# A SwiGLU feed-forward on one core: two products moved behind residual steps, and a fourth PSUM bank for the down product

## The chip, the cores and the metric

The kernel runs on one core of a Trainium2 chip. The metric is the device time of one execution in microseconds (us). Five engines work side by side: PE multiplies matrices (PEld is its weight load), DVE, ACT and POOL work element by element, and SP issues DMAs. PE writes its results into PSUM, which holds 8 banks of 128 partitions x 512 fp32 values; DVE and ACT read them from there.

## The reference, cut to what matters

The program is one decoder block: adaLN modulation, two token mixers (a gated recurrence and a dilated attention), an output projection, a SwiGLU feed-forward, and a final RMSNorm. SEQ is 2048, D_MODEL is 1024 and D_FF is 2816. The change touches the part from the feed-forward on (and one helper that the norms before it use as well):

```python
h = modulate(rms_norm(x, norm2_g[l]), shift2, scale2)
a, u = jnp.split(h @ w_gate_up[l], 2, axis=-1)
x = x + gate2[:, None, :] * ((jax.nn.silu(a) * u) @ w_down[l])
...
return rms_norm(x, final_g)
```

## The kernel before, in words

**Precision.** Every fp32 operand is split into a high part and a low part (`whi`, `wlo` for weights, `ahi`, `alo` for activations, `chi`, `clo` for the feed-forward's input), and a product is three matmuls: high x high, low x high, high x low. The weight split is a cast on ACT (L277) and a subtraction on POOL (L79, `wlo`).

**Blocks and pairs.** The 2048 tokens are cut into six blocks of 344 or 336 tokens (`n`), taken as three pairs (the loop `p`). The two blocks of a pair and the two halves of D_MODEL make a 2 x 2 block product, which `gate_up` computes with seven products instead of eight (a Strassen scheme); its sums and differences of the input are the `pieces` `h["11"]`, `h["S1"]` and so on, made by DVE and ACT.

**Columns and downs.** For each pair there are eleven steps `g`. Each runs `gate_up` for two columns of 128 gate and 128 up features. A column ends in `finish`, twice (once for each block): DVE multiplies silu(gate) by up (`tt(dve, si, si, u, ALU.mult)`, shown in the trace as DVE `hm<-hm`), and `two_parts` splits that product into `ahi` (ACT, L291) and `alo` (DVE). For the second column of a pair the splits are put into a list `late` and called later, inside the next `down`.

**The down product.** `down(g - 1, ...)` multiplies the two columns of the step before by the down weights. It has 16 steps, one for each 128-row tile of the output and each block. A step is six matmuls (L1123, L1124, L1125, twice) into one PSUM tile `psD`, and then one DVE instruction (L1126, the residual step) that reads `psD` and adds it into `xc`. The tag `psD` has three banks, so the fourth step's first matmul can only start when the residual step of the first has read its bank. In all there are 33 downs of 16 steps.

**The norms.** `norm_sum` (L296) sums squares over the partitions by a matmul with a matrix of ones into a PSUM tile `nps`, in a bank of its own. It serves the norms of the output projection, and the final norm: twice within the downs of the second and third pair, and twice in the last down. The products of `gate_up` have four banks (`psG`). Together that is all eight banks.

**Order.** The program is written in Python in one order, and a scheduler then puts each engine's instructions in an order of its own, by when it expects their inputs to be ready. Each engine then works through its list strictly in that order.

Of the kernel before, what the change touches and what calls it, by code (L numbers as in the profile page):

```python
# [10 lines left out]
F32 = mybir.dt.float32  # L11
# [4 lines left out]
ALU = mybir.AluOpType  # L16
# [3 lines left out]
P = 128  # L20
# [9 lines left out]
CH = 512  # L30
# [19 lines left out]
def hybrid_block(ctx, tc, xT, small, cst, w_ada, w_ft, w_tk, w_out, w_gu, w_dn, out):  # L50
    nc = tc.nc
    act, dve, pool, pe = nc.scalar, nc.vector, nc.gpsimd, nc.tensor
# [25 lines left out]
    def tt(eng, o, a, b, op):  # L78
        return eng.tensor_tensor(o, a, b, op)  # L79
# [173 lines left out]
    cpool, silu = {}, []  # L253

    def c_pool(name, stack=cx, **kw):
        cpool[name] = stack.enter_context(tc.tile_pool(name=name, bufs=1, reuse_waits="tile", **kw))
        return cpool[name]
# [11 lines left out]
    def raw_w(src):  # L269
        raw = cpool["wp"].tile([P, 512], F32, name="wraw", tag="wraw", bufs=7)  # L270
        nc.sync.dma_start(out=raw, in_=src)
        return raw
# [8 lines left out]
    def split(src, eng=pool):  # L281
        return [parts(raw_w(src[:, z * 512:(z + 1) * 512]), eng=eng) for z in range(2)]
# [6 lines left out]
    def two_parts(dst, src, eng=dve, copy=act.copy):  # L289
        hi, lo = dst  # L290
        copy(hi, src)  # L291
        tt(eng, lo, src, hi.bitcast(F32), ALU.subtract)

    def norm_sum(ssq, n):
        ps = cpool["pp_n"].tile([P, CH], F32, name="nps", tag="nps", bufs=1)[:, 0:n]
        pe.matmul(ps, ones, ssq, start=True, stop=True)  # L296
        return ps

# [26 lines left out]
    with ExitStack() as ab:  # L325
# [88 lines left out]
        with tc.tile_pool(name="ada0", bufs=2) as pl:  # L414
# [18 lines left out]
            with tc.manual_schedule(engines={mybir.EngineType.PE}):  # L433
              done = {}
              for k in range(KT + LAG0):
# [4 lines left out]
                  if 0 < k <= KT:  # L440
                      n = k - 1
# [435 lines left out]
    def product(ps, w, h, start=True, stop=True):  # L877

        for k, (hi, lo) in enumerate(h):
            ws = slice(k * P, (k + 1) * P)  # L880
            pe.matmul(ps, w[0][:, ws], hi, start=start and k == 0, stop=False, skip_group_check=True)  # L881
            pe.matmul(ps, w[0][:, ws], lo, start=False, stop=False, skip_group_check=True)  # L882
            last = pe.matmul(ps, w[1][:, ws], hi, start=False, stop=stop and k == 3, skip_group_check=True)  # L883
        return last.ins

    def psG(n):
        return cpool["ppc"].tile([P, CH], F32, name="psG", tag="psG", bufs=4)[:, 0:n]
# [45 lines left out]
    with ExitStack() as wl:  # L933
        for nm in ("hg1", "at0", "xw0", "xw1", "at1", "wsc"):
            c_pool(nm, wl)
        for nm in ("pp_d", "ppc", "pp_n"):
            c_pool(nm, space=PSUM)

        def w_tile(name, bufs=2):
# [39 lines left out]
        for i, (c, j) in enumerate(order):  # L979
# [5 lines left out]
            if begun:  # L985
                ps = begun.pop(0)
            else:
                ps = psG(CH)
# [26 lines left out]
            if c == NCH - 1:  # L1015
# [3 lines left out]
                if j == 1:  # L1019
                    n = BLK[0][1]  # L1020
# [13 lines left out]
    with cx:  # L1034
        for nm in ("wk_h", "wk_a", "wkc", "xpc0", "xpc1"):
            c_pool(nm)
        pp_d, wk_a = cpool["pp_d"], cpool["wk_a"]

        def hm(n):
            return cpool["wk_h"].tile([P, T], F32, name="hm", tag="hm", bufs=6)[:, 0:n]  # L1040

        def a_tile(n):
            return tuple(wk_a.tile([P, T], F32R, name=nm, tag=nm, bufs=8)[:, 0:n] for nm in ("ahi", "alo"))
# [9 lines left out]
        def gate_up(f, h, n, wait=False):  # L1053


            b11, b12 = raw_w(w_gu[f][:, 0:512]), raw_w(w_gu[FT + f][:, 0:512])
            b22, b21 = raw_w(w_gu[FT + f][:, 512:1024]), raw_w(w_gu[f][:, 512:1024])
            t1, t2 = [cpool["wk_h"].tile([P, 512], F32, name="wt", tag="wt", bufs=2) for _ in range(2)]
            e = [hm(n) for _ in range(4)]
            res, late = [], []  # L1060

            def finish(si, u):

                tt(dve, si, si, u, ALU.mult)
                res.append(a_tile(n))
                late.append(lambda: two_parts(dst, si))
                dst = res[-1]

            p11 = psG(n)
            product(p11, parts(b11), h["11"])  # L1070
            act.copy(e[0], p11)

            with tc.issue_after(pace[0]) if pace else nullcontext():
                tt(dve, t1, b12, b11, ALU.subtract)
                tt(dve, t2, b22, t1, ALU.subtract)

            p5 = psG(n)
            product(p5, parts(t1), h["S1"])
            p6 = psG(n)
            product(p6, parts(t2), h["S2"])  # L1080
            tt(dve, e[0], e[0], p6, ALU.add)
            tt(dve, b12, b22, b12, ALU.subtract)
            p7 = psG(n)
            product(p7, parts(b12), h["S3"])
            pace[:] = [tt(dve, e[1], e[0], p7, ALU.add).ins]
            tt(dve, e[2], e[1], p5, ALU.add)
            product(p11, parts(b21), h["12"], start=False)
            act.activation(e[3], p11, AF.Silu)
            tt(dve, b11, t2, b21, ALU.subtract)
            p4 = psG(n)  # L1090
            product(p4, parts(b11), h["22"])
            tt(dve, e[1], e[1], p4, ALU.subtract)
            silu[:] = [act.activation(e[1], e[1], AF.Silu).ins]
            product(p5, parts(b22), h["S4"], start=False)
            tt(dve, e[0], e[0], p5, ALU.add)
            finish(e[3], e[0])
            finish(e[1], e[2])
            if not wait:
                for f in late:
                    f()  # L1100
            return res, late

        def down(g, acts, xs, n, then=None, soon=(), extra=(), every=1):

            wd = {}

            def weights(jh):
                if jh not in wd:
                    wd[jh] = split(w_dn[g, jh])
                return wd[jh]  # L1110

            order = [(j, i) for i in range(2) for j in range(8)] if then else \
                [(j, i) for j in range(8) for i in range(2)]
            for step, (j, i) in enumerate(order):
                if step == 4:
                    for f in soon:
                        f()
                w, x = weights(j // 4), xs[i][:, j, :]
                ws = slice(j % 4 * P, (j % 4 + 1) * P)
                ps = pp_d.tile([P, CH], F32, name="psD", tag="psD", bufs=3)[:, 0:n]  # L1120
                for z in range(2):
                    ahi, alo = acts[z][i]
                    pe.matmul(ps, w[z][0][:, ws], ahi, start=z == 0, stop=False)  # L1123
                    pe.matmul(ps, w[z][0][:, ws], alo, start=False, stop=False)  # L1124
                    pe.matmul(ps, w[z][1][:, ws], ahi, start=False, stop=z == 1)  # L1125
                dve.scalar_tensor_tensor(x, ps, ga2[:, j:j + 1], x, ALU.mult, ALU.add)  # L1126
                if then:
                    then(i, j)
                if extra and step % every == every - 1:
                    extra.pop(0)()  # L1130
# [37 lines left out]
        for p in range(3):  # L1168
            n = BLK[2 * p][1]
            xs = load_blocks(p, x2_d)  # L1170
            steps = finish_steps(p - 1, *last) if p else []
            for g in range(11):
                acts = [gate_up(2 * g, h, n)[0]]
                a, late = gate_up(2 * g + 1, h, n, True)
# [94 lines left out]
```

## Time and profile before

| | |
|---|---|
| median of 3 runs | 3075.54 us (3074.14 to 3080.18) |
| the profiled execution | 3070.15 us |
| its span, from the first to the last instruction | 3068.4 us |
| PE busy | 2850.8 us, 93% of the span |
| DVE, ACT, POOL busy | 67%, 43%, 46% |
| mean granted TensorE clock | 0.979 of 2.4 GHz |

The profiled execution took 1.75 us more than its span, and lies 5.4 us below the median of the timed runs. Busy time of PE is the union of matmuls that are pipelined: a matmul of 344 columns is shown with 0.32 us, but the next one starts 0.16 us after it. Starts are therefore the measure of PE's pace below.

### The profile page before, as it was taken

The numbers are of one execution on the slowest core, as the hardware profiler recorded it, in microseconds if no ns is written. First come the engines' busy times: TensorE is split into PE (matmuls) and PEld (weight loads), VectorE is DVE, ScalarE is ACT, GpSimd is POOL, SyncE is SP. The second block draws the span as 40 slices with busy tenths as digits, with TensorE's granted clock in tenths as the row PEclk, the third lists the DMA queues.
The fourth block names the chain that finished last, engine by engine and source line by source line (L and its number), as shares of the span: only waits on it lengthen the run. The fifth ranks groups of instructions, "written<-read, shape, count | busy, mean of one in ns | idle before, by whom it ended". The sixth has DMA issues, their size and how long they took to land. (4 is left out here: it accounts for less than half of the span.)

```text
span 3068.4 us, 45120 instructions
## 1 busy us (share of the span) xinstructions
PE 2850.8 (93%) x16308; PEld 2595.3 (85%) x16308; DVE 2067.0 (67%) x3781; ACT 1312.5 (43%) x2388; POOL 1408.4 (46%) x1074
## 2 busy tenths in 40 slices
PE   6999998889899999998989999999999998999998
PEld 4777776667678999987769999998999998999997
DVE  7567566667644665666776666678667669776676
ACT  4533423334432565665554333345333335443334
POOL 5344422244533232320036566566566655665664
PEclk9999999999999999999989999999999999999999
DMA  6301336400238674537744222123232212231221
GB/s 243 118 35 42 117 124 219 151 32 32 83 115 218 143 165 101 134 106 237 260 161 157 73 80 79 60 83 106 96 116 73 80 66 95 83 113 63 81 71 67
DMA packets 212031, 343.32 MB, mean 112 GB/s; under 512 B 24784, under 2 KB 97360, under 8 KB 208720
## 3 DMA queue, kind: packets, MB, share of 16 engines
q1 hardware_dynamic: 201984, 322.35, 33.3%
q10 hardware_dynamic: 9824, 18.09, 1.6%
q8 instruction: 128, 2.10, 0.3%
q14 instruction: 95, 0.78, 0.1%
HBM read 281.39 MB, written 58.98 MB: 111 GB/s over the span
## 5 line engine op out<-in xcount | busy, mean ns | idle before, releaser
L79 POOL TENSOR_TENSOR wlo<-wraw,whi 128x512 fp32r<-128x512 f32 (+1 forms) x540 | 846.7, 1590 | 535.8 <-ACT whi L86 305.9
L881 PE MATMUL psG<-chi,whi 128*128 128x344 f32 (+1 forms) x1848 | 596.8, 323 | 15.6 <-DVE hm L79 7.4
L883 PE MATMUL psG<-chi,wlo 128*128 128x344 f32 (+1 forms) x1848 | 593.0, 321 | 3.5 <-POOL wlo L79 3.5
L882 PE MATMUL psG<-clo,whi 128*128 128x344 f32 (+1 forms) x1848 | 594.6, 322 | 0.0
L277 ACT CAST whi<-wraw 128x512 fp32r<-128x512 f32 x520 | 311.2, 619 | 423.7 <-issue 191.8
L1123 PE MATMUL psD<-ahi,whi 128*128 128x344 f32 (+1 forms) x1056 | 345.7, 327 | 43.8 <-DVE xc L1126 43.7
L1126 DVE SCALAR_TENSOR_TENSOR xc<-psD,mods,xc 128x344 f32<-128x344 f32 (+1 forms) x528 | 295.2, 569 | 110.0 <-PE psD L1125 109.8
L881 PEld LDWEIGHTS psG<-chi,whi 128*128 128x128 f32 x1848 | 351.2, 190 | 20.7 <-DVE hm L79 6.8
L883 PEld LDWEIGHTS psG<-chi,wlo 128*128 128x128 f32 x1848 | 350.5, 190 | 4.3 <-POOL wlo L79 4.1
L882 PEld LDWEIGHTS psG<-clo,whi 128*128 128x128 f32 x1848 | 350.2, 190 | 0.0
L79 POOL TENSOR_TENSOR wlo<-wt,whi 128x512 fp32r<-128x512 f32 x132 | 194.3, 1481 | 334.7 <-ACT whi L277 263.3
L1125 PE MATMUL psD<-ahi,wlo 128*128 128x344 f32 (+1 forms) x1056 | 337.3, 319 | 0.0
L1124 PE MATMUL psD<-alo,whi 128*128 128x344 f32 (+1 forms) x1056 | 336.3, 318 | 0.0
L79 DVE TENSOR_TENSOR hm<-hm,psG 128x344 f32<-128x344 f32 (+1 forms) x330 | 165.8, 503 | 244.3 <-PE psG L883 243.6
L511 PE MATMUL psA<-hhi,whi 128*128 128x512 f32 x640 | 262.7, 411 | 1.7 <-ACT hhi L396 1.7
L512 PE MATMUL psA<-hlo,whi 128*128 128x512 f32 x640 | 259.5, 406 | 0.2 <-DVE hlo L79 0.2
L513 PE MATMUL psA<-hhi,wlo 128*128 128x512 f32 x640 | 259.1, 405 | 0.0
L1123 PEld LDWEIGHTS psD<-ahi,whi 128*128 128x128 f32 x1056 | 198.8, 188 | 59.9 <-DVE xc L1126 55.5
L79 POOL TENSOR_TENSOR hd<-hb 128x256 f32<-128x256 f32 x192 | 134.2, 724 | 165.5 <-DVE hy L624 82.3
L1124 PEld LDWEIGHTS psD<-alo,whi 128*128 128x128 f32 x1056 | 199.0, 188 | 0.5
L1125 PEld LDWEIGHTS psD<-ahi,wlo 128*128 128x128 f32 x1056 | 198.9, 188 | 0.0
L277 ACT CAST whi<-wt 128x512 fp32r<-128x512 f32 x132 | 81.2, 617 | 258.9 <-DVE wt L79 139.0
(237 smaller groups left out, 6023.5 us busy)
## 6 DMA issues: line engine op xcount, KB each, us to landing
wraw<-in_w_gu SPq DMA_DIRECT2D x264, 256.0 KB
wraw<-in_w_dn SPq DMA_DIRECT2D x132, 256.0 KB
adaw<-in_w_ada SPq DMA_DIRECT2D x48, 512.0 KB
wraw<-in_w_ft SPq DMA_DIRECT2D x40, 512.0 KB
wraw<-in_w_tk SPq DMA_DIRECT2D x32, 512.0 KB
qk_d<-st SPq DMA_DIRECT2D x64, 256.0 KB
v<-v_d SPq DMA_DIRECT2D x16, 1024.0 KB
wraw<-in_w_out SPq DMA_DIRECT2D x64, 256.0 KB
```

The source lines that it names most:

```text
L79: return eng.tensor_tensor(o, a, b, op)
L277: copy(hi, raw)
L511: pe.matmul(ps, whi[:, ws], hhi[:, k, :], start=k == 0, stop=False)
L512: pe.matmul(ps, whi[:, ws], hlo[:, k, :], start=False, stop=False)
L513: pe.matmul(ps, wlo[:, ws], hhi[:, k, :], start=False, stop=k == 7)
L881: pe.matmul(ps, w[0][:, ws], hi, start=start and k == 0, stop=False, skip_group_check=True)
L882: pe.matmul(ps, w[0][:, ws], lo, start=False, stop=False, skip_group_check=True)
L883: last = pe.matmul(ps, w[1][:, ws], hi, start=False, stop=stop and k == 3, skip_group_check=True)
L1123: pe.matmul(ps, w[z][0][:, ws], ahi, start=z == 0, stop=False)
L1124: pe.matmul(ps, w[z][0][:, ws], alo, start=False, stop=False)
L1125: pe.matmul(ps, w[z][1][:, ws], ahi, start=False, stop=z == 1)
L1126: dve.scalar_tensor_tensor(x, ps, ga2[:, j:j + 1], x, ALU.mult, ALU.add)
```

## The change

`finish` in `gate_up` no longer issues the multiplication of silu(gate) by up itself. It puts it into the list `late`, ahead of the splits. For a first column nothing else changes, since its list is called at once. For a second column the list now has four entries (two multiplications, two splits). The `down` that gets the list used to call all of its entries ahead of its step 4 (counted from 0); now it calls one ahead of each of the steps 2, 3, 4 and 5. The tag `psD` gets a fourth bank, and `norm_sum` draws its tile from the same four banks instead of one of its own.

```diff
     def norm_sum(ssq, n):
-        ps = cpool["pp_n"].tile([P, CH], F32, name="nps", tag="nps", bufs=1)[:, 0:n]
+        ps = cpool["pp_d"].tile([P, CH], F32, name="nps", tag="psD", bufs=4)[:, 0:n]
...
-        for nm in ("pp_d", "ppc", "pp_n"):
+        for nm in ("pp_d", "ppc"):
             c_pool(nm, space=PSUM)
...
-            def finish(si, u):
-
-                tt(dve, si, si, u, ALU.mult)
-                res.append(a_tile(n))
-                late.append(lambda: two_parts(dst, si))
-                dst = res[-1]
+            def finish(i, si, u):
+
+                def mul():
+                    tt(dve, si, si, u, ALU.mult)
+                    res.append(a_tile(n))
+                late.insert(i, mul)
+                late.append(lambda: two_parts(res[i], si))
...
-            finish(e[3], e[0])
-            finish(e[1], e[2])
+            finish(0, e[3], e[0])
+            finish(1, e[1], e[2])
...
-                if step == 4:
-                    for f in soon:
-                        f()
+                if step > 1 and soon:
+                    soon.pop(0)()
...
-                ps = pp_d.tile([P, CH], F32, name="psD", tag="psD", bufs=3)[:, 0:n]
+                ps = pp_d.tile([P, CH], F32, name="psD", tag="psD", bufs=4)[:, 0:n]
```

**Place 1, a down in the middle of a pair.** PE's rows from the second matmul half of step 2 to the start of step 4 of the second down of the first pair, with what they wait for (the number behind a name tells one tile from another). Before:

```order
L1123 MATMUL psD_15746<-ahi_15255,whi_15726 128x344
L1124 MATMUL psD_15746<-alo_15256,whi_15726 128x344
L1125 MATMUL psD_15746<-ahi_15255,wlo_15727 128x344
L1123 MATMUL psD_15754<-ahi_15105,whi_15720 128x344 [waits DVE_49]
L1124 MATMUL psD_15754<-alo_15106,whi_15720 128x344
L1125 MATMUL psD_15754<-ahi_15105,wlo_15721 128x344
L1123 MATMUL psD_15754<-ahi_15258,whi_15726 128x344
L1124 MATMUL psD_15754<-alo_15259,whi_15726 128x344
L1125 MATMUL psD_15754<-ahi_15258,wlo_15727 128x344
L1123 MATMUL psD_15766<-ahi_15102,whi_15720 128x344 [waits DVE_49]
```

The same rows of the changed kernel:

```order
L1123 MATMUL psD_15740<-ahi_15280,whi_15717 128x344
L1124 MATMUL psD_15740<-alo_15281,whi_15717 128x344
L1125 MATMUL psD_15740<-ahi_15280,wlo_15718 128x344
L1123 MATMUL psD_15751<-ahi_15102,whi_15711 128x344
L1124 MATMUL psD_15751<-alo_15103,whi_15711 128x344
L1125 MATMUL psD_15751<-ahi_15102,wlo_15712 128x344
L1123 MATMUL psD_15751<-ahi_15291,whi_15717 128x344
L1124 MATMUL psD_15751<-alo_15292,whi_15717 128x344
L1125 MATMUL psD_15751<-ahi_15291,wlo_15718 128x344
L1123 MATMUL psD_15761<-ahi_15099,whi_15711 128x344 [waits DVE_49]
```

The order is the same; the first wait for DVE has moved from step 3 to step 4.

DVE's rows at the same place, from the last but one of the column's sums to the fourth residual step (`hm` are the column's sums and products, `xc<-psD` the residual steps). These are the rows of the kernel before:

```order
L79 TENSOR_TENSOR hm_15580<-hm_15580,hm_15581 128x344
L79 TENSOR_TENSOR hm_15579<-hm_15579,psG_15603 128x344
L79 TENSOR_TENSOR hm_15582<-hm_15582,hm_15579 128x344
L1126 SCALAR_TENSOR_TENSOR xc_14647<-psD_15730,mods_63,xc_14647 128x344
L79 TENSOR_TENSOR alo_15714<-hm_15582,ahi_15713 128x344
L1126 SCALAR_TENSOR_TENSOR xc_14648<-psD_15738,mods_63,xc_14648 128x344
L79 TENSOR_TENSOR alo_15717<-hm_15580,ahi_15716 128x344
L1126 SCALAR_TENSOR_TENSOR xc_14647<-psD_15746,mods_63,xc_14647 128x344
L1126 SCALAR_TENSOR_TENSOR xc_14648<-psD_15754,mods_63,xc_14648 128x344
```

And these are the rows of the changed kernel:

```order
L79 TENSOR_TENSOR hm_15577<-hm_15577,hm_15578 128x344
L79 TENSOR_TENSOR hm_15576<-hm_15576,psG_15600 128x344
L79 TENSOR_TENSOR hm_15579<-hm_15579,hm_15576 128x344
L1126 SCALAR_TENSOR_TENSOR xc_14644<-psD_15721,mods_63,xc_14644 128x344
L79 TENSOR_TENSOR alo_15739<-hm_15579,ahi_15738 128x344
L1126 SCALAR_TENSOR_TENSOR xc_14645<-psD_15729,mods_63,xc_14645 128x344
L79 TENSOR_TENSOR alo_15750<-hm_15577,ahi_15749 128x344
L1126 SCALAR_TENSOR_TENSOR xc_14644<-psD_15740,mods_63,xc_14644 128x344
L1126 SCALAR_TENSOR_TENSOR xc_14645<-psD_15751,mods_63,xc_14645 128x344
```

Nothing has moved: the scheduler puts both multiplications (the first and third row) ahead of the first residual step in both kernels. The orders of ACT, POOL and SP are the same here too. DVE's order differs at the ends of the first and second pair and in the last down alone; PE's too, but for waits as above.

**Place 2, the end of the first pair.** One piece of the difference in DVE's order, at the start of the last down but one of that pair (`clo<-hm`, `hm<-xc` and `xc<-xc` are pieces of the next pair's input):

```order
-L79 TENSOR_TENSOR hm<-hm 128x344
-L1126 SCALAR_TENSOR_TENSOR xc<-psD,mods,xc 128x344 x2
-L79 TENSOR_TENSOR alo<-hm,ahi 128x344
-L1126 SCALAR_TENSOR_TENSOR xc<-psD,mods,xc 128x344
-L79 TENSOR_TENSOR alo<-hm,ahi 128x344
+L1126 SCALAR_TENSOR_TENSOR xc<-psD,mods,xc 128x344
+L79 TENSOR_TENSOR hm<-hm 128x344
 L1126 SCALAR_TENSOR_TENSOR xc<-psD,mods,xc 128x344
 L79 TENSOR_TENSOR hm<-xc 128x344
 L1126 SCALAR_TENSOR_TENSOR xc<-psD,mods,xc 128x344
+L79 TENSOR_TENSOR alo<-hm,ahi 128x344
```

Here one multiplication does move behind the first residual step, and the splits behind it move back. In the last down of that pair PE's order changes as well: nine matmuls of the next pair's first product (`psG`) stood among its steps, the first ahead of step 2 and the last ahead of step 7. Now three do, ahead of steps 5 and 8, and six have moved behind the last step. At the end of the second pair it was seven, and now it is one.

**Place 3, the last down of the program.** PE's rows around the first of the two `nps` matmuls (`psD_30130` is step 7, the last of the first block). Before, the matmul stands within step 10:

```order
L1125 MATMUL psD_30190<-ahi_29715,wlo_30029 128x336
L296 MATMUL nps_30145<-ssq_30046,ones_68 128x336 [waits DVE_49]
L1123 MATMUL psD_30190<-ahi_29868,whi_30034 128x336
L1124 MATMUL psD_30190<-alo_29869,whi_30034 128x336
L1125 MATMUL psD_30190<-ahi_29868,wlo_30035 128x336
```

In the changed kernel it stands between step 7 and step 8:

```order
L1125 MATMUL psD_30130<-ahi_29890,wlo_30091 128x336
L296 MATMUL nps_30142<-ssq_30043,ones_68 128x336 [waits DVE_49]
L1123 MATMUL psD_30164<-ahi_29712,whi_30025 128x336
L1124 MATMUL psD_30164<-alo_29713,whi_30025 128x336
L1125 MATMUL psD_30164<-ahi_29712,wlo_30026 128x336
```

The matmul for the norm has moved ahead by two and a half steps, and with it its wait for DVE's sum of squares of the first block.

## Rows read from the trace of the kernel before

**Rows 1.** The page, engines: busy us (share of the span) xinstructions.
```profile
PE 2850.8 (93%) x16308; PEld 2595.3 (85%) x16308; DVE 2067.0 (67%) x3781; ACT 1312.5 (43%) x2388; POOL 1408.4 (46%) x1074
```

**Rows 2.** Waits of PE, 1650 us to the end: us, times, longest us.
```profile
PE psD L1123 <- DVE xc L1126: 43.7, 39, 2.4
PE psG L881 <- DVE hm L79: 7.4, 8, 2.4
PE nps L296 <- DVE ssq L79: 5.7, 1, 5.7
```

**Rows 3.** Timeline, second down: start us, us, engine line op tiles [idle before].
```profile
1701.81 0.32 PE L1123 MATMUL psD<-ahi,whi 128*128 128x344 f32 x1
...
1702.73 1.51 POOL L79 TENSOR_TENSOR wlo<-wt,whi 128x512 fp32r<-128x512 f32 x1 [0.37 <-ACT whi L277]
...
1702.75 0.32 PE L1123 MATMUL psD<-ahi,whi 128*128 128x344 f32 x1
...
1703.00 1.61 DVE L79 TENSOR_TENSOR hm<-hm 128x344 f32<-128x344 f32 x1
...
1704.47 0.32 PE L1125 MATMUL psD<-ahi,wlo 128*128 128x344 f32 x1
...
1705.07 0.52 DVE L79 TENSOR_TENSOR hm<-hm 128x344 f32<-128x344 f32 x1
1705.50 0.57 DVE L1126 SCALAR_TENSOR_TENSOR xc<-psD,mods,xc 128x344 f32<-128x344 f32 x1
...
1706.12 0.42 PE L1123 MATMUL psD<-ahi,whi 128*128 128x344 f32 x1 [1.33 <-DVE xc L1126]
...
1706.56 0.57 DVE L1126 SCALAR_TENSOR_TENSOR xc<-psD,mods,xc 128x344 f32<-128x344 f32 x1
...
1707.19 0.43 PE L1123 MATMUL psD<-ahi,whi 128*128 128x344 f32 x1
...
1709.38 0.58 DVE L1126 SCALAR_TENSOR_TENSOR xc<-psD,mods,xc 128x344 f32<-128x344 f32 x1 [0.37 <-PE psD L1125]
```

**Rows 4.** Waits of PE, 1700 to 2040 us, first pair.
```profile
PE psD L1123 <- DVE xc L1126: 10.5, 8, 1.3
```

**Rows 5.** Waits of PE, 2140 to 2530 us, second pair.
```profile
PE psD L1123 <- DVE xc L1126: 10.1, 11, 1.3
```

**Rows 6.** Waits of PE, 2630 to 3000 us, third pair.
```profile
PE psD L1123 <- DVE xc L1126: 14.2, 11, 2.3
```

**Rows 7.** Timeline of PE, second down of the second pair.
```profile
2193.72 0.42 PE L1123 MATMUL psD<-ahi,whi 128*128 128x344 f32 x1 [0.20 <-DVE xc L1126]
...
2195.24 0.42 PE L1123 MATMUL psD<-ahi,whi 128*128 128x344 f32 x1 [0.32 <-DVE xc L1126]
```

**Rows 8.** Timeline of PE, the program's first down.
```profile
1661.29 0.43 PE L1123 MATMUL psD<-ahi,whi 128*128 128x344 f32 x1 [1.96 <-DVE xc L1126]
```

**Rows 9.** Windows: length, busy us (xinstructions) of PE, PEld, DVE, ACT, POOL; PEclk, DMA.
```profile
1661.90:1665.20 3.30, 3.30 (x13) 3.30 (x13) 2.27 (x5) 0.00 (x0) 0.00 (x0) 0.50 0.00 0
1701.81:1717.00 15.19, 13.86 (x88) 13.44 (x87) 11.20 (x20) 2.84 (x6) 4.61 (x4) 1.00 0.10 34
2050.00:2069.00 19.00, 16.02 (x97) 14.87 (x96) 19.00 (x34) 8.90 (x21) 9.85 (x8) 1.00 0.17 58
2069.00:2090.00 21.00, 20.59 (x130) 20.08 (x129) 20.76 (x38) 11.20 (x23) 10.22 (x8) 1.00 0.40 121
2090.00:2117.00 27.00, 21.21 (x123) 19.60 (x122) 24.67 (x32) 18.57 (x40) 16.75 (x12) 0.98 0.29 90
```

**Rows 10.** Instructions of tile psD: count, duration ns min/median/max, first and last start.
```profile
L1126 DVE SCALAR_TENSOR_TENSOR xc<-psD,mods,xc x528: 550/569/579, 1660.7 to 3053.0; 128x344 f32<-128x344 f32 x118, 128x336 f32<-128x336 f32 x58
```

**Rows 11.** Timeline, the last down and the end.
```profile
3042.70 0.32 PE L1123 MATMUL psD<-ahi,whi 128*128 128x336 f32 x1
...
3043.62 0.32 PE L1123 MATMUL psD<-ahi,whi 128*128 128x336 f32 x1
...
3045.39 0.51 DVE L79 TENSOR_TENSOR ssq<-ssq,sq 128x336 f32<-128x336 f32 x1
...
3045.96 0.83 PE L296 MATMUL nps<-ssq,ones 128*128 128x336 f32 x2
...
3047.72 0.48 ACT L302 ACTIVATE ssq<-xc 128x336 f32<-128x336 f32 x1
...
3057.60 1.49 PE L296 MATMUL nps<-ssq,ones 128*128 128x336 f32 x2 [5.73 <-DVE ssq L79]
```

## The prediction

> **What bounds the kernel now.** I read the engines' table first, to see which engine can set the time: PE is busy for 93% of the span [rows 1]. From 1650 us on, where the feed-forward runs, I then read what PE waits for. Nearly all of it is one wait: the first matmul of a down step waits for the residual step of DVE that frees its bank, 39 times, 43.7 us in all [rows 2]. The third view is one down in order of time [rows 3]. Step 0 starts at 1701.81 and step 1 at 1702.75, so a step of six matmuls takes 0.94 us, and three banks hold 2.8 us of PE's work. DVE is late: one product took 1.61 us (1703.00), the other is done at 1705.59, and only then comes the first residual step, 1705.50 to 1706.07. PE has issued step 2's last matmul at 1704.47, could start step 3 some 0.16 us later, at 1704.63, and starts it at 1706.12. It loses 1.49 us, and 1.6 us by the time step 4 starts at 1707.19. After that DVE has caught up: it waits 0.37 us for PE ahead of each residual step. Outside such waits PE hardly stands still there, so what a down loses is lost by the whole program.
>
> **What the change does in a regular down.** The orders show that the diff's first half does nothing here: the scheduler had set both products ahead of the first residual step, and it still does, row for row. The work is the same too. I therefore cost the moved products at nothing, with the first residual step at its old time. What is left is the bank. PE's wait moves from step 3 to step 4: PE does step 3 at 1704.63, while DVE is late, and waits ahead of step 4 until 1706.12, the moment at which it used to start step 3. Step 5 needs the second residual step (1706.56 to 1707.13) and starts at 1707.19, where step 4 used to start [rows 3]. From there on PE is one step ahead of before. The gain is one step, 0.94 us, and about 0.6 us of the wait stays. It is not taken back within the down, because DVE needs 0.57 us for a residual step (550 to 579 ns in all 528 of them [rows 10]) where PE needs 0.94.
>
> **The sum.**
>
> - First pair, second to ninth down: 8 waits, 10.5 us, longest 1.3 [rows 4]. Second pair: 11 waits, 10.1 us [rows 5], of which four small ones belong to the two downs that carry a norm; the other 7 are like those of the first pair. 15 downs x 0.94 = 14.1 us.
> - Third pair: 11 waits, 14.2 us [rows 6], four small ones again. The other 7 are longer than a step, and its step is 0.92 us (3043.62 less 3042.70, two halves of 0.46 [rows 11]). 7 x 0.92 = 6.4 us.
> - The four downs with a norm wait twice, for 0.20 and 0.32 us by the rows [rows 7]. These idle times count from a matmul's shown end, which lies 0.16 us behind its slot (1.33 us stood for 1.49 above), so 0.36 and 0.48 us are lost, and some 0.1 us each time at the slower start behind it (0.42 us for 0.32). One bank more covers nearly all of that 1.0 us, but no more than a step: 4 x 0.93 = 3.7 us. The norm's tile now takes a bank of the ring. Its matmul stands where it stood, and ACT reads it long before the fourth tile behind it needs that bank, so I cost this at nothing; if ACT came late, one step would wait.
> - The program's first down waits 1.96 us [rows 8], and behind that wait the granted clock is 0.50, the lower of its two levels (1.2 GHz), for 3.3 us [rows 9]. That costs half of it, 1.65 us, beside the step. In the regular downs, which wait 1.3 us, the clock stays at 1.00 [rows 9]. Here about 1.2 us of the wait is left, so I expect the clock to stay up. Bounds: 0.94 (the clock falls all the same) and 2.6 us; DVE's next residual steps cap it, and I take 2.2. The Trainium skill, page "TensorE: Matmul & The Clock Gate", section "Part 1: The HAM clock gate", says that the low clock is the default and that sustained activity lifts it. By that rule a shorter wait should help, and this row agrees; but waits of up to 2.4 us elsewhere [rows 2] left the clock at 1.00 [rows 9], so the length of a wait alone doesn't decide it.
> - The last but one down of the third pair waits little: 0.3 us.
> - The two ends of pairs, 2044 to 2117 us and its like near 2550. DVE is busy 19.0 of 19.0, 20.8 of 21.0 and 24.7 of 27.0 us there [rows 9]: the pieces of the next pair run on it, with the old residual steps and the squares. What PE wins in these downs it mostly waits for later, at the next pair's first columns. At most DVE's own idle time can be won, some 2.6 us each. On the other side, six of the matmuls that filled PE's waits now stand behind the down: 6 x 0.16 = 1.0 us could be lost, with a late sum or two 1.4. I take +0.5 each, 1.0 us, nearer to zero since DVE's work is unchanged.
> - The last down. The first norm's matmul now stands behind step 7, and waits there for the sum of squares, which ends at 3045.90 [rows 11]. PE could have gone on at 3043.62, so it loses 2.3 us. Queued behind it are steps 8 to 15, and for these DVE's residual steps and ACT's squares. But ACT used to start on the second block's squares only at 3047.72 [rows 11], being busy with the first block's norm, and the end hangs on DVE's and ACT's chain of sums until 3057.60, not on PE. The first residual step of the second block now comes at about that time, so I take -0.4 us; the bounds are 0 and -2.3.
>
> Together: 14.1 + 6.4 + 3.7 + 2.2 + 0.3 + 1.0 - 0.4 = 27.3 us. Against the profiled execution this gives 3070.15 - 27.3 = 3042.9 us. The median of the runs lies 5.4 us above that execution, and the same difference carried over gives **3048.2 us**. ACT and POOL prepare weights as PE frees their buffers, so they move with PE; POOL is busy for 4.6 of 15.2 us of a down [rows 9], so I see no new bound there.
>
> **The rivals.**
>
> *The bank buys nothing, as DVE is the bound (no change).* If DVE did not catch up within a down, a further bank would let PE run ahead once and then wait as before. The ends of pairs speak for it, with DVE busy throughout; the regular downs speak against it, with DVE waiting 0.37 us for PE at each later step [rows 3]. The time would be that of before less what the first down gives, 3070 to 3075 us. The Trainium skill, "TensorE: Matmul & The Clock Gate", section "HAM oscillation — how this bites in real kernels", tells of a kernel where a second PSUM buffer brought nothing further. By that case the time would stay at some 3075 us; here the wait is named and short, which that page does not say of its own kernel. Chance 0.05.
>
> *Collisions on DVE (slower).* The product of 1.61 us ran while POOL worked on a weight's low part (1702.73 to 1704.24); the other one, with POOL idle, took 0.52 [rows 3]. The difference is 1.09 us. PE's head start from step 3 on lets ACT and POOL prepare weights about a step earlier; should POOL then meet the second product or the sums ahead of the first residual step as well, each down would lose 1.1 us per collision. One more collision in each of the 27 downs costs 29 us and cancels the gain (about 3078), and two make it 3107. Against it: POOL's work at that place is started by PE's earlier products, which the change doesn't move, and the residual steps themselves are never slowed [rows 10]. The Trainium skill, "SBUF — State Buffer", section "Who interferes with whom", says that a DVE instruction with two SBUF inputs contends with a GpSimd instruction that reads SBUF, and one with a single such input does not; the two durations agree. Chance 0.02.
>
> *Half of it is given back.* The ends of pairs and the tail take their bounds (2 x -1.4 and -2.3) and something else of about 4 us, such as weights that come late behind a faster down. That leaves 16 to 20 us: 3056 to 3060 us. Chance 0.10.
>
> *More.* The ends of pairs win DVE's idle time (2 x 2.6) and the first down its full 2.6: 32 us or more, about 3043 and below. Chance 0.06.
>
> *My forecast*, a gain of 20 to 32 us: 0.77.
>
> **How the numbers follow.** From the forecast's terms at their bounds: first down 0.94, ends of pairs -2.8, tail -2.3 give a gain of 20.3 us, 3055.2; the upper bounds give 32.3 us, 3043.2. The median of three runs can itself be off by one or two us (they spread over 6), so the range is 3042 to 3056; it leaves out the other cases, some 0.2. A difference of 0.2%, 6.2 us, is about what a measurement of this kernel tells from no change. Faster: forecast, half and more, 0.77 + 0.10 + 0.06 = 0.93. Same: 0.05. Slower: 0.02.
>
> **What would show it.** In the profile after, regular downs should show PE's wait at the fifth step's first matmul, of 0.4 to 0.6 us instead of 1.3, with DVE's product of 1.6 us and the first residual step unmoved, and columns that follow each other some 0.94 us sooner. PE's waits for residual steps should fall from 43.7 us to about 20. The clock should be 1.00 near 1662 us. In the last down PE should stand some 2 us ahead of the first norm's matmul, with the last one hardly later against the down's start. I am wrong if the first residual steps start much later than 3.7 us after a down's start (1705.50 less 1701.81 before), or if waits for weights (`whi`, `wlo`) or for `hm` appear where there are none now.

## The result, and the profile after

The changed kernel takes 3042.2 us (median of 4 runs, 3039.56 to 3046.21) where the kernel before took 3074.84 us beside it (4 runs, 3073.5 to 3080.18). The ratio is 0.9896 [0.9879, 0.9913], which is 26.8 to 37.2 us saved. The prediction was 3048.2 us, range 3042.0 to 3056.0: the direction is right, and the time lies 0.2 us inside the range's lower edge. The profiled execution of the changed kernel took 3046.21 us, the longest of its four, with a span of 3044.4 us. Against the profiled execution of before (3070.15 us) that is 23.9 us less, where the sum said 27.3.

The engines' table of the page has hardly changed against [rows 1]: PE does the same work, and only the time in which it did none is shorter.

```profile
PE 2850.2 (94%) x16308; PEld 2594.9 (85%) x16308; DVE 2060.8 (68%) x3781; ACT 1313.1 (43%) x2388; POOL 1405.5 (46%) x1074
```

PE's waits from 1650 us to the end (us, times, longest us) answer to [rows 2]:

```profile
PE psD L1123 <- DVE xc L1126: 17.9, 33, 1.8
PE psG L881 <- DVE hm L79: 11.1, 8, 2.4
PE nps L296 <- DVE ssq L79: 4.9, 2, 2.7
PE psG L881 <- ACT hm L1072: 0.9, 1, 0.9
PE psG L883 <- POOL wlo L79: 0.5, 1, 0.5
```

Beside those of [rows 2], the kernel before had two more:

```profile
PE psG L881 <- ACT sq L305: 3.0, 2, 1.8
PE psG L881 <- ACT hm L1071: 1.5, 2, 0.9
```

The wait for residual steps is down from 43.7 to 17.9 us. The next columns' products (`psG`) wait about as long as before: 3.7 us more for DVE's sums (7.4 before), 3.6 us less for ACT, and once, new, 0.5 us for POOL's low part of a weight. All of these lie at the ends of the pairs.

The timeline of the second down, on PE, POOL and DVE, answers to [rows 3]:

```profile
1701.10 0.32 PE L1123 MATMUL psD<-ahi,whi 128*128 128x344 f32 x1
...
1702.00 1.50 POOL L79 TENSOR_TENSOR wlo<-wt,whi 128x512 fp32r<-128x512 f32 x1 [0.38 <-ACT whi L277]
...
1702.27 1.61 DVE L79 TENSOR_TENSOR hm<-hm 128x344 f32<-128x344 f32 x1
...
1704.33 0.52 DVE L79 TENSOR_TENSOR hm<-hm 128x344 f32<-128x344 f32 x1
...
1704.71 0.32 PE L1125 MATMUL psD<-ahi,wlo 128*128 128x344 f32 x1
1704.77 0.57 DVE L1126 SCALAR_TENSOR_TENSOR xc<-psD,mods,xc 128x344 f32<-128x344 f32 x1
...
1705.39 0.43 PE L1123 MATMUL psD<-ahi,whi 128*128 128x344 f32 x1 [0.36 <-DVE xc L1126]
```

DVE does at the same distance from the down's start what it did before: the slow product at 1.17 us, the first residual step at 3.67 us (3.69 before). PE goes on to the end of step 3 (1704.71) and then waits 0.36 us of idle time, where it waited 1.33 us ahead of step 3. Step 4 starts 4.29 us after the down's start; step 3 started at 4.31 us before. That is the one step.

The clock, in windows of the first down just behind its wait, of the second down, of the third pair's first down just behind its wait, and of the last down behind the first norm's wait (length, busy us of PE, PEld, DVE, ACT, POOL; PEclk is the granted clock as a share of 2.4 GHz):

```profile
1662.94:1666.30 3.36, 3.35 (x20) 3.22 (x21) 3.35 (x8) 0.36 (x1) 0.00 (x0) 1.00 0.00 0
1701.10:1717.00 15.90, 15.54 (x99) 15.12 (x98) 12.11 (x21) 3.27 (x7) 4.57 (x4) 1.00 0.11 32
2622.64:2626.00 3.36, 3.36 (x14) 3.36 (x14) 2.72 (x7) 0.00 (x0) 0.00 (x0) 0.50 0.00 0
3021.90:3025.30 3.40, 3.40 (x14) 3.40 (x13) 0.57 (x1) 2.60 (x5) 1.69 (x2) 0.50 0.00 0
```

The low stretch behind the program's first down [rows 9] is gone. New ones stand in the third pair's first down and in the last down.

### The profile page after: what moved, and what is told of

The parts are those of the page before. It is cut to its first block, busy times and chain, and to the rows that moved or that the text cites. A ratio compares the mean times of both kernels' runs of the same rounds, so it can differ in the third digit from the quotient of the medians.

```text
span 3044.4 us, 45120 instructions
## 1 busy us (share of the span) xinstructions
PE 2850.2 (94%) x16308; PEld 2594.9 (85%) x16308; DVE 2060.8 (68%) x3781; ACT 1313.1 (43%) x2388; POOL 1405.5 (46%) x1074
## 5 line engine op out<-in xcount | busy, mean ns | idle before, releaser
L1123 PE MATMUL psD<-ahi,whi 128*128 128x344 f32 (+1 forms) x1056 | 346.5, 328 | 18.4 <-DVE xc L1126 17.9
```

## Experiments

All kernels of the first group ran on one chip with the kernel before (23 runs, median 3073.73 us), those of the second group likewise (9 runs, 3073.01 us). In the table I took from each trace the start of the first `psD` matmul of each down (downs counted from 1 to 33), and write the time from one such start to another, in us of the profiled execution. "Tied" is the experiment below in which DVE's order is fixed.

| from the start of down | before | after | bank alone | products alone | tied | tied, 3 banks |
|---|---|---|---|---|---|---|
| 1 to 2 | 45.48 | 43.55 | 43.35 | 45.71 | 41.70 | 42.24 |
| 2 to 10 (first pair) | 348.23 | 340.65 | 340.68 | 348.31 | 334.81 | 334.81 |
| 10 to 12 (end of the first pair) | 97.13 | 96.90 | 96.47 | 96.75 | 97.34 | 97.17 |
| 12 to 21 (second pair) | 391.41 | 382.95 | 383.74 | 391.54 | 377.59 | 377.59 |
| 21 to 23 (end of the second pair) | 95.84 | 94.90 | 95.77 | 95.90 | 93.93 | 95.89 |
| 23 to 24 | 43.57 | 44.49 | 42.13 | 43.57 | 42.05 | 42.55 |
| 24 to 32 (third pair) | 343.05 | 335.71 | 335.63 | 343.09 | 327.67 | 328.72 |
| 32 to 33 | 15.22 | 14.77 | 14.77 | 15.21 | 14.77 | 14.77 |
| 33 to the end | 32.10 | 32.96 | 32.27 | 32.23 | 32.53 | 32.37 |
| 1 to the end | 1412.03 | 1386.88 | 1384.81 | 1412.32 | 1362.38 | 1366.11 |

**The two kernels once more (c1_before_again, c1_after_again).** Both unchanged, to see what a difference between two executions means.

> The kernel before, unchanged, as a measure of how far two executions of one program differ. Ratio 1.000 within 0.2%. From the first down's first matmul to the end 1412.1 us in the earlier profile (3068.4 less 1656.3); I expect 1412 +- 2 here. The start of that first down lay at 1656.3 in the profile of before and at 1657.6 in that of the changed kernel, whose instructions are the same up to there but for a wait: I expect it to move by up to 5 us between executions. If so, the measured 33 us between the medians are 25 us of the downs and some scatter of the stages ahead of them. Rival: the stages ahead keep to within 1 us, and then the changed kernel must gain something there that I have not seen.

> The changed kernel, unchanged, in five more rounds. My theory (each of 26 downs gains one step of 0.92 to 0.94 us, ends of pairs and tail next to nothing) gives 25 to 28 us, ratio 0.9909 to 0.9919. Rival: something outside the downs gives 6 us more, ratio 0.989. From the first down to the end 1386.9 us in the earlier profile; 1387 +- 3 here.

Before again: 3071.53 us (12 runs, 3066.28 to 3077.89), ratio 0.9998 [0.9983, 1.0013]. After again: 3041.11 us (6 runs, 3036.17 to 3049.96), ratio 0.9906 [0.9886, 0.9926], 22.7 to 35.0 us. From the first down's start to the end the traces repeat within about 1 us (1412.57 against 1412.03; 1385.84 against 1386.88). What does not repeat lies ahead of it. The ratio of after again, 0.9906, lies just below the 0.9909 to 0.9919 that I expected; its interval holds both this and the rival's 0.989. The row of `psD`'s first matmuls (duration in ns, first and last start) of after and of after again:

```profile
L1123 PE MATMUL psD<-ahi,whi x1056: 310/319/644, 1657.5 to 3030.3; 128*128 128x344 f32 x118, 128*128 128x336 f32 x58
```

```profile
L1123 PE MATMUL psD<-ahi,whi x1056: 310/319/582, 1651.0 to 3023.3; 128*128 128x344 f32 x118, 128*128 128x336 f32 x58
```

The same program reaches its first down 6.5 us sooner in one execution than in the other, which is more than the 5 us that I expected; over the ten traces of this case the first down starts between 1651.0 and 1663.4 us. A gain is therefore better read from the downs on than from two spans.

**The bank alone (c1_bank_only).** The kernel before with the fourth bank and the norms' tile in it; the products stay as they were.

```diff
-        ps = cpool["pp_n"].tile([P, CH], F32, name="nps", tag="nps", bufs=1)[:, 0:n]
+        ps = cpool["pp_d"].tile([P, CH], F32, name="nps", tag="psD", bufs=4)[:, 0:n]
...
-                ps = pp_d.tile([P, CH], F32, name="psD", tag="psD", bufs=3)[:, 0:n]
+                ps = pp_d.tile([P, CH], F32, name="psD", tag="psD", bufs=4)[:, 0:n]
```

> The fourth bank, shared with the norms, alone; the products are issued as in the kernel before. My theory says that the bank is the whole of the change: first down to end 1387 +- 3 us, waits of 0.5 us ahead of step 4 in the regular downs, ratio to before 0.9909 to 0.9919, as the changed kernel within 2 us. Rival (putting the products off does half of it): 1400 us, ratio 0.9955.

3042.95 us (6 runs, 3038.09 to 3047.87), ratio 0.9909 [0.9891, 0.9926]: as much as the whole change, by the runs. By the traces it is 1 to 2 us ahead of it from the first down on (1384.81 against 1386.88 and 1385.84). PE's waits, from 1650 us on:

```profile
PE psD L1123 <- DVE xc L1126: 18.7, 33, 1.5
```

**The products alone (c1_products_only).** The diff's other half: `finish` and the calls in `down` as in the changed kernel, three banks, and the norm's bank of its own.

```diff
+                def mul():
+                    tt(dve, si, si, u, ALU.mult)
+                    res.append(a_tile(n))
+                late.insert(i, mul)
...
+                if step > 1 and soon:
+                    soon.pop(0)()
```

> The products put off in the program's text, three banks for the down and the norms' own bank as before. My theory: the scheduler leaves both products ahead of the first residual step, so nothing changes: 1412 +- 2 us from the first down to the end, waits of 1.3 us ahead of step 3, ratio 1.000 within 0.1%. Rival (putting the products off does half of it): 1400 us, ratio 0.9955.

3075.27 us (12 runs, 3066.48 to 3080.88), ratio 1.0005 [0.9991, 1.0018]: nothing. Its waits, and the wait of its second down, are those of before:

```profile
PE psD L1123 <- DVE xc L1126: 42.6, 40, 2.3
```

```profile
1708.05 0.42 PE L1123 MATMUL psD<-ahi,whi 128*128 128x344 f32 x1 [1.31 <-DVE xc L1126]
```

**The order tied (c2_forced).** The changed kernel, with each call of the list tied behind the residual step before it, so that the scheduler can no longer put the products ahead.

```diff
-                    soon.pop(0)()
+                    with tc.issue_after(res): soon.pop(0)()
...
-                dve.scalar_tensor_tensor(x, ps, ga2[:, j:j + 1], x, ALU.mult, ALU.add)
+                res = dve.scalar_tensor_tensor(x, ps, ga2[:, j:j + 1], x, ALU.mult, ALU.add).ins
```

> The changed kernel, with each of the four late entries tied behind the residual step ahead of it, so that DVE's order in the regular downs is: two residual steps, product, residual step, product, residual step, split, residual step, split. My theory: what is left of the wait (0.75 us in 15 downs, 0.9 in 7, 0.2 in 4, 1.7 in the first) comes from the products alone, of which one takes 1.6 us; the first residual step should end about 2.3 us after the down's start instead of 4.25, and no step should wait. From the first down to the end 1367 +- 4 us (1385 to 1387 with the changed kernel), ratio to before 0.983 to 0.986. Rival: the slow product only moves, makes the second or third residual step late by as much, or the splits late for the next down; then no more than 5 us are won, ratio 0.989 or above.

3024.08 us (4 runs, 3022.51 to 3025.61), ratio 0.9841 [0.9826, 0.9855]; another 24.5 us from the first down to the end. At 1362.38 us that stretch is 0.6 us shorter than the lower end of what I expected. The timeline of its second down, which starts at 1700.84 (POOL and DVE):

```profile
1701.75 1.51 POOL L79 TENSOR_TENSOR wlo<-wt,whi 128x512 fp32r<-128x512 f32 x1 [0.37 <-ACT whi L277]
1702.02 0.51 DVE L79 TENSOR_TENSOR hm<-hm,psG 128x344 f32<-128x344 f32 x1
1702.45 1.05 DVE L1126 SCALAR_TENSOR_TENSOR xc<-psD,mods,xc 128x344 f32<-128x344 f32 x2
1703.42 0.51 DVE L79 TENSOR_TENSOR hm<-hm 128x344 f32<-128x344 f32 x1
1703.86 0.58 DVE L1126 SCALAR_TENSOR_TENSOR xc<-psD,mods,xc 128x344 f32<-128x344 f32 x1
```

The first residual step starts 1.61 us after the down's start (3.67 in the changed kernel). The first two residual steps now run beside POOL's `wlo`, unslowed, and the product comes when POOL is done and takes 0.51 us, where it took 1.61. So of the 2.06 us by which the first residual step comes sooner, about 1.1 are this collision; the rest is the plain time of the products that no longer stand ahead of it. In the groups of the whole program (busy us, mean ns of one), the 132 products in the changed kernel and in this one:

```profile
L79 DVE TENSOR_TENSOR hm<-hm 128x344 f32<-128x344 f32 (+1 forms) x132 | 115.3, 873 | 21.2 <-ACT hm L1094 19.1
```

```profile
L79 DVE TENSOR_TENSOR hm<-hm 128x344 f32<-128x344 f32 (+1 forms) x132 | 92.3, 700 | 19.7 <-ACT hm L1094 18.5
```

**The order tied, with three banks (c2_forced_3banks).** As above, with `bufs=3` for `psD` and a bank for the norms alone.

```diff
-        ps = cpool["pp_d"].tile([P, CH], F32, name="nps", tag="psD", bufs=4)[:, 0:n]
+        ps = cpool["pp_n"].tile([P, CH], F32, name="nps", tag="nps", bufs=1)[:, 0:n]
...
-                ps = pp_d.tile([P, CH], F32, name="psD", tag="psD", bufs=4)[:, 0:n]
+                ps = pp_d.tile([P, CH], F32, name="psD", tag="psD", bufs=3)[:, 0:n]
```

> The same forced order with three banks for the down and the norms' own bank, as before. My theory: a fourth bank only covers DVE's lateness. With the first residual step done at 2.3 us, ahead of step 3's start at 2.8, three banks nearly do: the slow product behind the second residual step delays the third to about 4.7 us and step 5 (due at 4.7) hardly waits. From the first down to the end 1367 to 1375 us, ratio 0.983 to 0.988: the order alone is worth more than the bank alone (1385 us, 0.991). Rival: the bank is needed in any order; then waits of 0.5 us or more stay in each regular down, and the time is 1385 us or more.

3027.26 us (4 runs, 3022.71 to 3030.34), ratio 0.985 [0.9833, 0.9866]. The two intervals overlap, so the runs don't tell it from four banks; the traces put the difference at 3.7 us (1366.11 less 1362.38). Here too the stretch is shorter than the 1367 to 1375 us that I expected. In the first two pairs the two are alike to the hundredth (334.81 and 377.59). PE's waits from 1650 us on with three banks:

```profile
PE psD L1123 <- DVE xc L1126: 7.0, 12, 1.4
```

And with four:

```profile
PE psD L1123 <- DVE xc L1126: 3.8, 8, 0.9
```

So a fourth bank is worth some 27 us while DVE is late (1412.03 less 1384.81), and 3.7 us once DVE is not. The order is worth 46 us with three banks (1412.32 less 1366.11).

**The final norm in another ring (c2_norm_in_gate_ring, c2_forced_norm_in_gate_ring).** The changed kernel, and the tied one, with the final norm's tiles taken from the four banks of `psG`. That is so for all six of them: the two of the last down, where these banks lie idle, and the four inside the downs of the second and third pair, where `gate_up` uses them too. Only the norms ahead of the feed-forward stay with `psD`.

```diff
-    def norm_sum(ssq, n):
-        ps = cpool["pp_d"].tile([P, CH], F32, name="nps", tag="psD", bufs=4)[:, 0:n]
+    def norm_sum(ssq, n, ring=("pp_d", "psD")):
+        ps = cpool[ring[0]].tile([P, CH], F32, name="nps", tag=ring[1], bufs=4)[:, 0:n]
...
-            ps = norm_sum(box["ssq"], n)
+            ps = norm_sum(box["ssq"], n, ("ppc", "psG"))
```

> The changed kernel, but the final norm's tiles come from the four banks of the gate and up products instead of the down's. PE's first matmul for the norm stands within step 10 of the last down again, as before. My theory: PE no longer waits 2.4 us ahead of step 8 (7.. excess 3.9 us falls to 0.4), but the program's end hangs on DVE's and ACT's sums, so the last down to the end falls only from 32.3 to 33.0 us back to 32.1 to 32.2 (as before): 0 to -0.8 us. Rival: PE's wait passes through to the end; then the last down to the end falls by 2 us or more below 31 us.

> The forced order, four banks for the down, and the final norm's tiles from the gate and up ring. If both theories hold it is the fastest: 1366 +- 4 us from the first down to the end, some 0.5 us below the forced order alone, ratio 0.983 to 0.986. Rival: none of its own; it shows whether the two edits add up.

On the changed kernel: 3043.54 us (4 runs, 3038.37 to 3050.88), ratio 0.9906 [0.9886, 0.9926], which is no difference. On the tied one: 3018.73 us (5 runs, 3011.86 to 3025.35), ratio 0.9823 [0.9803, 0.9842]. It is the fastest kernel measured here and beats both kernels of the change; that it also beats the tied kernel is not shown, since the intervals overlap (1361.81 against 1362.38 us from the first down on, just below the 1362 to 1370 that I expected). The four norms inside the downs make no difference in either ring: from down 12 to 21 it is 383.02 us on the changed kernel, 382.95 without the edit. The end of the changed kernel, where the last down starts at 3011.47 (PE and ACT; `nps` is the norm's matmul):

```profile
3021.15 0.83 PE L296 MATMUL nps<-ssq,ones 128*128 128x336 f32 x2 [2.16 <-DVE ssq L79]
...
3024.25 0.49 ACT L302 ACTIVATE ssq<-xc 128x336 f32<-128x336 f32 x1 [0.72 <-DVE xc L1126]
...
3033.63 0.83 PE L296 MATMUL nps<-ssq,ones 128*128 128x336 f32 x2 [2.71 <-DVE ssq L79]
```

And with the final norm's tile in the other ring:

```profile
3026.72 0.83 PE L296 MATMUL nps<-ssq,ones 128*128 128x336 f32 x2
...
3028.48 0.48 ACT L302 ACTIVATE ssq<-xc 128x336 f32<-128x336 f32 x1
...
3038.36 1.49 PE L296 MATMUL nps<-ssq,ones 128*128 128x336 f32 x2 [5.73 <-DVE ssq L79]
```

The wait ahead of the first matmul is gone, and ACT starts on the second block without the 0.72 us of idle time. The last norm's matmul starts 21.34 us behind the last down's start (3017.03), as in the kernel before (3057.60 less 3036.26), where the changed kernel has 22.16. From the last down's start to the end it is 32.07 us, against 32.96 and 32.34 in the two executions of the changed kernel.

## Why the prediction was right, and where its sum was off

Term by term, from the table:

- **The regular downs and those with a norm** (15 plain, four with a norm, six of the third pair's seven): predicted 14.1 + 3.7 + 6 x 0.92 = 23.3 us. Measured, from the rows 2 to 10, 12 to 21 and 24 to 32: 7.58 + 8.46 + 7.34 = 23.4 us. With three banks the products cost nothing and brought nothing there (products alone: 348.31 against 348.23). It is one step of PE in each down, and of the wait 0.52 us are left (0.36 of idle time and the 0.16 by which a matmul's shown end lies behind its slot), where about 0.6 was forecast.
- **The first down:** predicted 2.2, measured 1.93, and 2.18 in the second execution. The granted clock stayed at 1.00 behind the shorter wait, as predicted. That is 0.94 us for the step and 1.43 for the steps behind the wait that ran at the lower clock (1.65 by the sum), less 0.44 because the first residual step ended later in this execution (5.34 us behind the down's start, 4.90 before).
- **The ends of pairs:** predicted 1.0 for both, measured 0.23 + 0.94 = 1.2 us. That this fits is partly luck: the +0.5 for each was a choice between wide bounds, and with the bank alone the same two ends gave 0.66 and 0.07 us. The 0.94 us of the second were given back at once, in the next item.
- **The third pair's first down** (23) is the term that was mis-sized. It stood in "7 x 0.92" and cost 0.92 us instead of gaining it.
- **The last but one down:** predicted 0.3, measured 0.45.
- **The last down:** predicted -0.4, measured -0.86, and -0.24 in the second execution. PE stood 2.16 us of idle time ahead of the first norm, as worked out, and little of it reached the end: the last norm's matmul starts 0.82 us later against the down's start, and the experiment that takes the wait away gains 0.3 to 0.9 us.

Together 25.2 us from the first down on (26.2 in the second execution), against 27.3. The 1.8 us of down 23 are nearly all of the difference; the other misses nearly cancel.

One of the signs that I had named for being wrong did appear, but not in the regular downs: PE waited once for a `wlo`, 0.5 us, and longer than before for DVE's `hm`, both at the ends of pairs.

**Down 23.** It has the longest wait of the regular downs ([rows 6], 2.3 us), and I took it for the same wait as theirs. POOL's, DVE's and PE's rows there (not all of them), in the changed kernel, where the down starts at 2616.50:

```profile
2609.59 8.89 POOL L79 TENSOR_TENSOR wlo<-wraw,whi 128x512 fp32r<-128x512 f32 x6 [0.67 <-ACT whi L277]
2618.45 1.29 POOL L79 TENSOR_TENSOR wlo<-wt,whi 128x512 fp32r<-128x512 f32 x1
...
2618.52 1.77 DVE L79 TENSOR_TENSOR wraw<-wt,wraw 128x512 f32<-128x512 f32 x1 [2.01 <-POOL wlo L79]
...
2621.59 0.56 DVE L1126 SCALAR_TENSOR_TENSOR xc<-psD,mods,xc 128x336 f32<-128x336 f32 x1
...
2622.20 0.42 PE L1123 MATMUL psD<-ahi,whi 128*128 128x336 f32 x1 [1.84 <-DVE xc L1126]
```

And with the bank alone, where the down starts at 2616.52:

```profile
2608.65 8.88 POOL L79 TENSOR_TENSOR wlo<-wraw,whi 128x512 fp32r<-128x512 f32 x6 [0.66 <-ACT whi L277]
2617.90 1.50 POOL L79 TENSOR_TENSOR wlo<-wt,whi 128x512 fp32r<-128x512 f32 x1 [0.37 <-ACT whi L277]
...
2620.65 0.56 DVE L1126 SCALAR_TENSOR_TENSOR xc<-psD,mods,xc 128x336 f32<-128x336 f32 x1
...
2621.27 0.42 PE L1123 MATMUL psD<-ahi,whi 128*128 128x336 f32 x1 [0.88 <-DVE xc L1126]
```

In the kernel before, where the down starts at 2634.42, DVE waits for POOL too:

```profile
2636.03 1.77 DVE L79 TENSOR_TENSOR wraw<-wt,wraw 128x512 f32<-128x512 f32 x1 [2.02 <-POOL wlo L79]
```

At the start of the third pair POOL is behind. It works on seven weights' low parts with hardly a pause, DVE waits 2.01 us for one of them ahead of the column's last sums, and the residual step and PE come behind that. "I see no new bound there" left this out.

POOL has its own pace: counted from the start of down 21, its run of six begins at 88.0 us in the changed kernel (2609.59 less 2521.60) and at 87.9 with the bank alone (2608.65 less 2520.75). PE reaches down 23 after 94.90 us in the one and 95.77 in the other. The moved products thus brought PE 0.87 us ahead at the end of the pair, and it met POOL's late work: the wait is 0.96 us longer (1.84 less 0.88). That would have been even, but behind the longer wait the granted clock fell to 0.50 for 3.4 us (the window above), which cost 1.4 us, the excess of the steps behind the wait over those in the kernel before. From down 21 to 24 it is 139.39 us, 139.41 before, and 137.90 with the bank alone. The products, which I costed at nothing, have their price at this place.

At the second pair's first down (12) it is the other way round. There it is the bank alone that meets POOL, with a down that starts at 2137.01:

```profile
2138.53 1.76 DVE L79 TENSOR_TENSOR wraw<-wt,wraw 128x512 f32<-128x512 f32 x1 [2.01 <-POOL wlo L79]
```

Its down 12 takes 43.33 us, as before (43.34), and 42.45 in the changed kernel. That is why the row 12 to 21 is 0.8 us longer with the bank alone.

**The median.** The medians lie 32.6 us apart in the first comparison, and by the larger set of runs 22.7 to 35.0 us. The downs gave 25 to 27 us. What goes beyond that goes with the granted clock, whose mean is on record for each run. In the 23 runs of the kernel before, the time follows it, from 3063.32 us at 0.983 to 3082.5 and 3087.1 at 0.975. At one and the same clock the two kernels lie as far apart as the downs say: at 0.982 two runs of the kernel before took 3065.87 and 3066.91 us and three of the changed kernel 3036.17, 3038.31 and 3043.62, and at 0.979 six took 3070.81 to 3074.95 us and two 3046.3 and 3049.96. That is 27.0 and 24.5 us between the means. The four runs of the first comparison had 0.980 to 0.982, the profiled execution of before 0.979. From the first down on the traces repeat within about 1 us, so this scatter is put down to the part ahead of it, where PE's order is the same in the two kernels and the ten traces differ by up to 12 us. Whether the changed kernel got the higher clock more often by chance is not shown.

I had carried over the 5.4 us by which the profiled execution of before lay below its median; that of the changed kernel lay 4.0 us above its own. So most of the 6.0 us by which 3048.2 was too high is scatter between executions and no term of the sum. The forecast is right by its mechanism and, but for one term, by its sum; that 3042.2 still lies in the range, by 0.2 us, is luck.

**The rivals.** That the bank buys nothing falls with the bank alone (0.9909). That half is given back falls too, since 25.2 us reach the end, and that collisions make it slower likewise: the first residual step stands at 3.67 us, unmoved. By the medians alone the 32.6 us would belong to the case "more", 32 us and above, but what this case was built on did not come: the ends of pairs won 0.23 and 0.94 us instead of 2.6 each, and the first down 1.93 instead of 2.6. The Trainium skill, "TensorE: Matmul & The Clock Gate", section "HAM oscillation — how this bites in real kernels", tells of a second PSUM buffer that brought nothing further. Here both cases were seen: the bank brought 27 us where the reader of the bank was late, and 3.7 us where it was not.

**The cause behind the wait.** The bank does not make DVE punctual; it lets PE run one step further. DVE was late because a product with two SBUF inputs stood ahead of the first residual step while POOL was reading. The Trainium skill, "SBUF — State Buffer", section "Who interferes with whom", says that such an instruction contends with a GpSimd instruction that reads SBUF, and one with at most one SBUF input does not; this case's rows agree (1.61 against 0.51 us for the product, 0.57 for the residual step beside POOL). The change's text meant to move the products, the scheduler put them back, and in the regular downs only the tied order did what the text says.

## What to carry to other kernels

A further buffer covers a late reader by one step, so its worth here was the smaller of one step and the wait, per repeat; look first why the reader is late, because an order that makes it punctual was worth 46 us here, and the bank on top of it 3.7. Where a scheduler sets the order, a move in the text may change nothing: compare the engines' orders, and tie the instructions if it must hold. Look apart at the first repeat of each group, where another engine may be the late one, and compare stretches of two traces rather than their totals, since the same program scattered by several us ahead of the changed part.

## What the runs showed of the hardware

The length of a wait alone does not tell whether the clock falls. In the first down, 1.96 us of idle time were followed by a granted clock of 0.50 [rows 8, 9], and 1.46 us in the changed kernel were not:

```profile
1662.94 0.42 PE L1123 MATMUL psD<-ahi,whi 128*128 128x344 f32 x1 [1.46 <-DVE xc L1126]
```

In down 23, 1.84 us were followed by 0.50 in the changed kernel. So were 1.83 us in its second execution, and 1.87 us with the final norm in the other ring. The 2.33 us of the kernel before, at the same place, were not: there the clock stayed at 1.00 (first the wait, then the window around it).

```profile
2639.70 0.42 PE L1123 MATMUL psD<-ahi,whi 128*128 128x336 f32 x1 [2.33 <-DVE xc L1126]
```

```profile
2638.00:2643.00 5.00, 3.30 (x20) 3.17 (x21) 4.54 (x11) 0.84 (x2) 0.00 (x0) 1.00 0.00 0
```

PE had run from the down's start to the wait without a gap in both. By the Trainium skill, "TensorE: Matmul & The Clock Gate", section "Part 1: The HAM clock gate", sustained activity lifts the clock, so less waiting should have helped. The first down agrees; down 23 went the other way, and why stays open.

The scatter of one program on one core was larger than I had taken it for: 3063.32 to 3087.1 us in 23 runs of the kernel before, with mean granted clocks from 0.983 down to 0.975.
